# Paired rounded root sums in layer 0, and the small softmax operations taken several blocks at a time

## The chip, the cores and the metric

The kernel runs on one core of one Trainium2 chip. The metric is the device time of one execution in microseconds (us). Three runs of the kernel before took 2031.17 to 2031.62 us, median 2031.27 us. One further execution was recorded by the hardware profiler; it took 2031.74 us.

Names used below: PE is the matrix engine (TensorE) and PEld its loading of weights, DVE is VectorE, ACT is ScalarE, POOL is GpSimd, and SP is the engine that issues most DMAs. L428 means line 428 of the kernel in question; line numbers of the kernel before and of the changed one differ behind line 690.

## The reference

A decoder trunk of two layers on 1024 tokens of width 1024, in float32. Each layer normalizes its input, projects it once, and hands the columns to four mixers:

```python
for l in range(DEPTH):
    h = rmsnorm(x, attn_norm[l])
    proj = h @ w_in[l]
    (c_q, c_kv, k_r, g_b, g_c, u_conv, u_pool, q_sw, k_sw, v_sw) = jnp.split(proj, pts, axis=-1)
    y_a = mla_attention(...)       # 4 heads, causal over all tokens
    y_b = short_gated_conv(...)
    y_c = multiscale_pool(...)
    y_d = swa_sink_attention(...)  # 4 heads, window of 128, a sink logit per head
    groups = jnp.stack([y_a, y_b, y_c, y_d], axis=2)
    # each group normalized by its own root mean square, then one output projection
    x = x + mixed @ w_o[l]
    h2 = rmsnorm(x, ffn_norm[l])
    gate, up = jnp.split(h2 @ w_gate_up[l], 2, axis=-1)
    x = x + (jax.nn.silu(gate) * up) @ w_down[l]
return rmsnorm(x, final_norm)

def rmsnorm(x, g):
    y = xf * lax.rsqrt(jnp.mean(xf * xf, axis=-1, keepdims=True) + RMS_EPS)
```

Two pieces matter here. Every `rmsnorm` (and the norm of each group) needs the sum of squares over channels for each token. And both attentions end in a softmax over keys; in the local one the sink joins the denominator: exp(sink - max) is added to the sum of the row.

## The kernel before

**Data.** Activations stand with channels on the 128 partitions and tokens along the free dimension, in two halves of 512 tokens (`t` = 0, 1). A product in float32 precision is made of three matmuls on operands rounded to the fast float32 format: each operand is split into a rounded part and a rest, and `mm3` (L348) adds high x high, high x low and low x high into one PSUM bank. The split itself is `split` (L368 on ACT copies and rounds, L371 on DVE subtracts; L373 and L374 do the same with a gain). `half_split` makes such a pair for one half of the tokens.

**Root sums.** The class `SumSq` collects squares of the channel blocks into one tile per half (`add`: the square on ACT, L412, the addition on DVE, L414 and L420). `rnorm` then sums over partitions with a matmul against a matrix of ones and forms the reciprocal root (L437 to L443 on ACT and DVE). It has two forms (L428 and L431). If the object was made with `pair`, the last `add` splits the collected tile into a rounded pair, and `rnorm` uses two matmuls in the fast format:

```python
            if t in self.hl:
                for i, h in enumerate(self.hl.pop(t)):
                    pe.matmul(p, ones_r, R.ap(h), start=i == 0, stop=i == 1)
                    R.free(h)
            else:
                pe.matmul(p, ones, a, start=True, stop=final is None)
```

Otherwise it uses one matmul in plain float32. Before the change, layer 0 uses the plain form for its input norm (`ss`), the norm of the query rank (`sq_q`) and the norms of the groups c (pooling) and d (local attention); everything else is paired but for the last half of the final norm.

**Local attention.** For each of two pairs of heads (`g`) and each of eight blocks of 128 queries (`i`), `swa_unit` makes the scores of two heads against two blocks of keys (L685), adds the bias and takes the row's negative maximum (L695, a custom DVE operation), takes Exp with row sums on ACT (L708), and then, for the two heads of that block, makes the sink's part (L718 on DVE, L719 Exp on ACT), adds it (L720) and takes the reciprocal (L721). Then the rows are scaled (L723), transposed by PE (L734), split, and multiplied with the values (L746). `swa_some` calls units in between the projections, three or two at a time.

**Latent attention.** There are eight steps, one for each head `h` and half `t`. `scores` handles the four query blocks of a step: scores into PSUM (L1071 to L1073), maxima (L1076, L1079), Exp with row sums on ACT (L1090, L1093), for `t` = 1 the sum of the two partial row sums (L1102), a reciprocal (L1103), and the scaling of the rows (L1107 on ACT, L1109 on DVE). `mix_values` transposes the rows (L1125) and multiplies them with the values (L1137); it is called one step later, behind the scores of the next step.

**Order.** The program is written once in plain order, recorded, and then ordered anew by a list scheduler in the kernel (class `Order`): it gives every instruction a cost and its dependences, ranks them, and fixes an order on each engine, and with it the PSUM bank of each product and the place of each temporary. A change in the recorded instructions so moves the order of the whole program.

Of the kernel before, what the change touches and what calls it, by code (L numbers as in the profile page):

```python
# [16 lines left out]
AF = mybir.ActivationFunctionType  # L17
ALU = mybir.AluOpType
AX = mybir.AxisListType

P = 128
D = 1024
# [3 lines left out]
NK = D // P  # L26
# [100 lines left out]
def trunk_kernel(ctx: ExitStack, tc: tile.TileContext, ins, out, given=None, ends=None):  # L127
    nc = tc.nc
    act, dve, pe, pool, sp = nc.scalar, nc.vector, nc.tensor, nc.gpsimd, nc.sync
# [61 lines left out]
    def small(n):  # L191
        return spool.tile([P, n], F32, name=f"sm{n}", tag=f"sm{n}", bufs=16 if n < 16 else 2)
# [262 lines left out]
    tl = slice(64, 128)  # L455

    x_in = ins["xT"]
    ss = SumSq(D)
    hh = [[None, None] for _ in range(NK)]
    xf = [[None, None] for _ in range(NK)]  # L460
    ratt = [None, None]
# [56 lines left out]
    for l in range(L):  # L518
# [57 lines left out]
        if l == 0:  # L576
# [44 lines left out]
            for i in range(L):  # L621
                for o, c, n in ((nsink, PC_SINK, 4), (nffn, PC_FFN, NK)):
                    dve.tensor_scalar(
                        out=o[:, i * n : i * n + n],
                        in0=par[:, i * PC_N + c : i * PC_N + c + n],
                        scalar1=-1.0,
                        scalar2=None,
                        op0=ALU.mult,
# [27 lines left out]
        for t in range(2):  # L656
            f = tmp()
            mul_to(f, pv_[t], r_of(t))
            p = ps("t")
# [3 lines left out]
            for g in range(2):  # L663
# [3 lines left out]
                    out=o[:, :, 1, :], in0=pv[:, :, g, :], in1=rd(o[:, :, 0, :]), op=ALU.subtract  # L667
# [3 lines left out]
        ytiles("d")  # L671
        psy_of = {}

        def swa_unit(g, i):

            t, b = divmod(i, 4)
            lo_k = max(i - 1, 0) * P
            nkb = 2 if i else 1
            c0 = 0 if i else P
            p = ps("s")  # L680
            s3 = p.rearrange("p (h k) -> p h k", h=2)
            for h in range(2):
                q = R.ap(qs[2 * g + h][t])[:, b * P : (b + 1) * P]
                for n in range(2):
                    pe.matmul(  # L685
                        s3[:, h, c0:],
                        q,
                        R.ap2(kk[g][n])[:, lo_k : lo_k + nkb * P],
                        start=n == 0,
                        stop=n == 1,  # L690
                    )
            nm, rs = small(2), small(2)
            for h in range(2):
                c = CC_SWA + (2 * g + h) * 256
                dve.tensor_tensor_reduce(  # L695
                    out=s3[:, h, c0:],
                    in0=s3[:, h, c0:],
                    in1=cst[:, c + c0 : c + 256],
                    scale=-1.0,
                    scalar=nsink[:, l * 4 + 2 * g + h : l * 4 + 2 * g + h + 1],  # L700
                    op0=ALU.add,
                    op1=ALU.min,
                    accum_out=nm[:, h : h + 1],
                )
            pr = tmp("tp")
            p3 = pr.rearrange("p (h k) -> p h k", h=2)
            for h in range(2):
                act.activation(  # L708
                    p3[:, h, c0:],
                    s3[:, h, c0:],  # L710
                    AF.Exp,
                    bias=nm[:, h : h + 1],
                    scale=-1.0,
                    accum_out=rs[:, h : h + 1],
                )
            es = small(2)
            sk = par[:, l * PC_N + PC_SINK + 2 * g : l * PC_N + PC_SINK + 2 * g + 2]
            dve.tensor_tensor(out=es, in0=nm, in1=sk, op=ALU.add)  # L718
            act.activation(es, es, AF.Exp)  # L719
            dve.tensor_tensor(out=rs, in0=rs, in1=es, op=ALU.add)  # L720
            dve.reciprocal(rs, rs)  # L721
            for h in range(2):
                dve.tensor_scalar(  # L723
                    out=p3[:, h, c0:],
                    in0=p3[:, h, c0:],
                    scalar1=rs[:, h : h + 1],
                    scalar2=None,
                    op0=ALU.mult,
                )
            pt = ps("t")  # L730
            ptv = pt.rearrange("p (b h q) -> p b h q", b=2, h=2)
            for kb in range(2 - nkb, 2):
                for h in range(2):
                    pe.transpose(ptv[:, kb, h, :], p3[:, h, kb * P : (kb + 1) * P], ident)  # L734
            a0 = (2 - nkb) * 256
            th, tlo = R.half(), R.half()
            split(R.ap(th)[:, a0:], R.ap(tlo)[:, a0:], pt[:, a0:])
            if i % 2 == 0:
                psy_of[g] = ps("pv")
            py = psy_of[g]  # L740
            n = 0
            for kb in range(2 - nkb, 2):
                j = i - 1 + kb
                v = R.ap(vs[g][j // 4])[:, (j % 4) * P : (j % 4 + 1) * P]
                for tt in (th, tlo):
                    pe.matmul(  # L746
                        py[:, (i % 2) * 256 : (i % 2 + 1) * 256],
                        v,
                        R.ap(tt)[:, kb * 256 : (kb + 1) * 256],
                        start=n == 0,  # L750
                        stop=n == 2 * nkb - 1,
                    )
                    n += 1
            R.free(th)
            R.free(tlo)
            if i % 2:
                pyv = py.rearrange("p (i h q) -> p i h q", i=2, h=2)
                tt = tmp("tn")
                for h, rows in ((0, hd), (1, tl)):
                    tv = tt[rows, 0:256].rearrange("p (i q) -> p i q", i=2)  # L760
                    o = F.ap(y["d"][g][t])[rows, (b - 1) * P : (b + 1) * P]
                    act.copy(tv, pyv[tl, :, h, :])
                    dve.tensor_tensor(
                        out=o.rearrange("p (i q) -> p i q", i=2),
                        in0=pyv[hd, :, h, :],
                        in1=tv,
                        op=ALU.add,
                    )

        units = deque((g, i) for g in range(2) for i in range(NK))  # L770

        def swa_some(n):
            for _ in range(n):
                if units and qs[2 * units[0][0]][1] is not None:
                    g, i = units.popleft()
                    swa_unit(g, i)
                    if i == NK - 1:
                        for h in range(2):
                            for t in range(2):
                                R.free(qs[2 * g + h][t])  # L780
                        for n2 in range(2):
                            R.free_pair(kk[g][n2])
                            R.free(vs[g][n2])

        def group_scale(g):

            sg = SumSq(2 * P, g in ("b", "bcd")[l])
            for t in range(2):
                for c in range(2):
                    sg.add(t, F.ap(y[g][c][t]))  # L790
                r = sg.rnorm(t)
                for c in range(2):
                    a = F.ap(y[g][c][t])
                    mul_to(a, a, F.ap(r))
                F.free(r)
# [59 lines left out]
        for ct in range(2):  # L855
            pp = nextp
            u, a, b = F.pair(), F.pair(), F.pair()
# [16 lines left out]
            else:  # L874
# [7 lines left out]
                out=dst,  # L882
                in0=src,
                scalar=cst[:, CC_INVW + ct : CC_INVW + ct + 1],
                in1=uf,
                op0=ALU.mult,
# [7 lines left out]
            for t in range(2):  # L894
                h, lo = half_split(dst[:, t * HT : (t + 1) * HT])
                p = ps("t")
# [15 lines left out]
                rope.append(F.half())  # L912
                sp.dma_start(F.ap(rope[-1]), ins[name][:, t * HT : (t + 1) * HT])
        cq = [[None, None], [None, None]]
        sq_q = SumSq(2 * P, l > 0)
        for m in range(2):
            pp = project() if m else nextp
            for t in range(2):
# [20 lines left out]
        for t in range(2):  # L939
            p = ps("s")  # L940
# [17 lines left out]
            p = ps("t")  # L958
# [88 lines left out]
        def scores(h, t, q):  # L1047
            pr = []
            own = [F.half(), F.half(), F.half()]

            diag = ((own[0], 0), (own[1], 0), (own[0], P), (own[2], 0))
            for b in range(4):
                i = 4 * t + b
                bs = slice(b * P, (b + 1) * P)
                nch = t + 1
                wd = (b + 1) * P
                s, c = diag[b]
                chunks = [F.ap(s)[:, c : c + wd]]
                if t:
                    own.append(F.half())  # L1060
                    chunks.insert(0, F.ap(own[-1]))
                rs = small(2)
                nm = small(1)
                pts = []
                for c in range(nch):
                    w_ = HT if c < t else max((b + 1) * P, 256)
                    p = ps("s")
# [6 lines left out]
                if nch == 2:  # L1074
# [5 lines left out]
                    out=pts[t][:, :wd],  # L1080
# [17 lines left out]
                    scale=-1.0,  # L1098
                    accum_out=rs[:, 0:1],
                )  # L1100
                if nch == 2:
                    dve.tensor_tensor(out=rs[:, 0:1], in0=rs[:, 0:1], in1=rs[:, 1:2], op=ALU.add)  # L1102
                dve.reciprocal(rs[:, 0:1], rs[:, 0:1])  # L1103
                for c in range(nch):
                    a = chunks[c]
                    if c < t and b % 2:
                        act.activation(a, a, AF.Copy, scale=rs[:, 0:1])  # L1107
                        continue
                    dve.tensor_scalar(  # L1109
                        out=a, in0=a, scalar1=rs[:, 0:1], scalar2=None, op0=ALU.mult  # L1110
                    )
                pr.append(chunks)
            R.free(q[0])
            R.free(q[1])
            return pr, own
# [594 lines left out]
        for f in range(3, NFF):  # L1710
# [5 lines left out]
            if f % 2:  # L1716
                g = f // 2
# [682 lines left out]
```

## Time and profile before

| | |
|---|---|
| median of three runs | 2031.27 us |
| profiled execution | 2031.74 us, its span 2030.0 us |
| PE busy | 2018.6 us (99%) |
| DVE busy | 1531.2 us (75%) |
| ACT busy | 1022.6 us (50%) |
| POOL busy | 567.5 us (28%) |
| mean granted clock of PE | 0.999 |

The span runs from the first to the last instruction; the execution's own time holds 1.7 us more around it. The mixers of layer 0 lie between 0 and about 380 us, its feed-forward part up to about 1050 us, the mixers of layer 1 between 1050 and 1400 us, and its feed-forward part behind them. A busy PE means that matmuls are under way, not that they start at the greatest pace: ends of matmuls are modelled, so what one costs is read from the distance between starts. The mean of a group of DVE or ACT operations is the duration of one, and two that follow one another may overlap in part. Waits are inferred from semaphores; where a wait is for several, the last one is named.

### The profile page before, as it was taken

What the parts mean: (1) busy time and instruction counts of PE and PEld (TensorE: products, weight loads), DVE (VectorE), ACT (ScalarE), POOL (GpSimd) and SP (SyncE); (2) the same over time, 40 slices, a digit from 0 to 9 for tenths busy, and PEclk for the clock granted to TensorE, in tenths of its full rate; (3) what the DMA queues carried; (4) which work ended last, traced back from release to release, by engine and by line L of the source; (5) the groups of instructions that cost most, each with busy time, mean ns of one, the idle gap of its engine ahead of it and who ended that gap; (6) DMA issues with size and microseconds to landing.
All of it is one profiled execution on the core that took longest, in us unless ns stands there. A gap on an engine that the chain in (4) does not pass through costs nothing.

```text
span 2030.0 us, 26831 instructions
## 1 busy us (share of the span) xinstructions
PE 2018.6 (99%) x9418; PEld 1676.7 (83%) x9418; DVE 1531.2 (75%) x2442; ACT 1022.6 (50%) x1778; POOL 567.5 (28%) x428
## 2 busy tenths in 40 slices
PE   9999999999999999999999999999999999999998
PEld 7888888888888888888888888888888888888887
DVE  8779989997666678776646998799976766785554
ACT  7447657843333335555633676677333333354343
POOL 0100000057776772000001000000587677710000
PEclk9999999999999999999999999999999999999999
DMA  5431132336445547998835224332554554487552
GB/s 207 109 63 55 64 108 81 136 131 205 169 164 201 175 163 266 354 371 283 296 100 133 63 91 133 105 126 93 175 168 169 199 172 169 162 301 259 190 178 84
DMA packets 154232, 338.57 MB, mean 167 GB/s; under 512 B 14960, under 2 KB 62192, under 8 KB 154096
## 3 DMA queue, kind: packets, MB, share of 16 engines
q1 hardware_dynamic: 149616, 325.31, 46.6%
q0 software_dynamic: 4480, 11.54, 3.2%
q8 instruction: 74, 1.21, 0.2%
q14 instruction: 62, 0.51, 0.1%
HBM read 241.36 MB, written 105.91 MB: 171 GB/s over the span
## 4 chain that ended last, share of the span: by engine, by line
PE 96%; DVE 0%; DMA 0%; ACT 0%; issue 0%; DVEq 0%; ACTq 0%
PE ps_mm L348 37%; PE ps_s L348 30%; PE ps_t L348 12%; PE ps_pv L348 8%; PE ps_pv L1137 2%; PE ps_t L1125 1%; PE ps_s L1071 1%; PE ps_s L1072 1%; PE ps_s L1073 1%; PE ps_s L685 1%; PE ps_s L943 1%; PE ps_pv L746 1%; PE ps_t L734 1%; PE ps_t L428 0%; DMA xp<-u 0%; PE ps_t L431 0%
## 5 line engine op out<-in xcount | busy, mean ns | idle before, releaser
L348 PE MATMUL ps_mm<-u,u 128*128 128x512 f32 (+1 forms) x3378 | 833.2, 390 | 0.5 <-ACT u L368 0.3
L348 PEld LDWEIGHTS ps_mm<-u,u 128*128 128x128 f32 x3378 | 614.6, 188 | 122.7 <-issue 2.6
L371 DVE TENSOR_TENSOR u<-u,u 128x1024 fp32r<-128x1024 f32 (+3 forms) x453 | 511.3, 1148 | 194.1 <-ACT u L368 176.5
L348 PE MATMUL ps_s<-u,u 128*128 128x512 f32 x2670 | 634.0, 389 | 0.0
L348 PEld LDWEIGHTS ps_s<-u,u 128*128 128x128 f32 x2670 | 501.0, 188 | 104.9 <-issue 0.5
L368 ACT CAST u<-u 128x1024 fp32r<-128x1024 f32 (+3 forms) x453 | 385.2, 868 | 382.9 <-DMA u<-ad 73.9
L348 PE MATMUL ps_t<-u,u 128*128 128x512 f32 (+1 forms) x1124 | 254.4, 377 | 0.0
L348 PEld LDWEIGHTS ps_t<-u,u 128*128 128x128 f32 x1124 | 202.7, 188 | 39.3 <-issue 0.5
L1548 POOL TENSOR_TENSOR tm<-tm,u 128x512 f32<-128x512 f32 x80 | 139.5, 1744 | 341.6 <-ACT tm L1546 337.1
L348 PE MATMUL ps_pv<-u,u 128*128 128x512 f32 x744 | 177.5, 389 | 0.0
L348 PEld LDWEIGHTS ps_pv<-u,u 128*128 128x128 f32 x744 | 139.5, 188 | 29.1 <-ACT u L1364 0.2
L322 POOL DMA_DIRECT2D gd<-in_w_gu x24 | 21.6, 898 | 415.0 <-PE ps_t L348 281.4
L1134 POOL MEMSET u<- 128x128 f32 x32 | 6.1, 217 | 428.7 <-PE ps_mm L348 193.5
L1546 ACT ACTIVATE tm<-tm 128x512 f32<-128x512 f32 x80 | 50.6, 632 | 135.8 <-DVE tm L449 135.7
L368 ACT CAST u<-ps_t 128x512 fp32r<-128x512 f32 (+3 forms) x132 | 65.8, 504 | 54.1 <-PE ps_t L1125 27.0
L371 DVE TENSOR_TENSOR u<-ps_t,u 128x512 fp32r<-128x512 f32 (+3 forms) x132 | 75.7, 582 | 18.9 <-ACT u L368 17.2
L1414 ACT COPY tm<-ps_s 128x512 f32<-128x512 f32 x61 | 35.8, 587 | 101.7 <-PE ps_s L348 101.6
L1626 POOL TENSOR_TENSOR u<-u,u 128x352 f32<-128x352 f32 x64 | 81.4, 1272 | 1.4
L412 ACT ACTIVATE tm<-u 128x512 f32<-128x512 f32 (+1 forms) x91 | 53.9, 600 | 49.2 <-DVE u L1817 41.2
L373 ACT ACTIVATE u<-u,par 128x512 fp32r<-128x512 f32 x99 | 69.4, 715 | 17.8 <-DVE u L1274 7.6
L1626 POOL TENSOR_TENSOR u<-u 128x352 f32<-128x352 f32 x64 | 75.4, 1180 | 3.0 <-DMA u<-in_w_dn 2.8
L374 DVE SCALAR_TENSOR_TENSOR u<-u,par,u 128x512 fp32r<-128x512 f32 x99 | 72.5, 745 | 4.4 <-ACT u L373 4.1
(206 smaller groups left out, 2316.3 us busy)
## 6 DMA issues: line engine op xcount, KB each, us to landing
u<-in_w_gu SPq DMA_DIRECT2D x84, 512.0 KB, 4.1
ad<-u SPq DMA_DIRECT2D x154, 256.0 KB, 3.2
u<-ad SPq DMA_DIRECT2D x70, 512.0 KB, 5.9
u<-in_w_dn SPq DMA_DIRECT2D x64, 352.0 KB, 3.4
qd<-u SPq DMA_DIRECT2D x64, 352.0 KB, 2.5
u<-in_w_in SPq DMA_DIRECT2D x43, 512.0 KB, 5.8
u<-qd SPq DMA_DIRECT2D x32, 512.0 KB, 5.4
u<-in_w_dn SPq DMA_DIRECT2D x24, 512.0 KB, 5.4
```

What stands on the lines that cost most here:

```text
L322: paced(pool.dma_start(d, a, **more))
L348: last_mm = pe.matmul(o, w, r, start=start and k == 0 and i == 0, stop=stop and k == n - 1 and i == 2, skip_group_check=again,)
L368: a = act.copy(hi, f)
L371: dve.tensor_tensor(out=lo, in0=f, in1=rd(hi), op=ALU.subtract)
L373: a = act.activation(hi, f, AF.Copy, scale=gain)
L374: dve.scalar_tensor_tensor(out=lo, in0=f, scalar=gain, in1=rd(hi), op0=ALU.mult, op1=ALU.subtract)
L412: act.activation(q, f, AF.Square)
L1137: pe.matmul(py[:, c0:], v_of(j, h), R.ap(s)[:, c0:], start=j == 0 and n == 0, stop=j == nj - 1 and n == 1,)
L1414: act.copy(o, p)
L1546: last_silu = act.activation(g, g, AF.Silu)
L1548: pool.tensor_tensor(out=g, in0=g, in1=r, op=ALU.mult)
L1626: pool.tensor_tensor(out=o, in0=a, in1=b, op=ALU.add)
```

## The change

Three places change what is computed in which instruction; the result is the same sum, maximum and quotient.

- In layer 0 the input norm, the query norm and the norms of groups c and d use the paired form of the root sum.
- In the local attention two neighbouring blocks are one unit: `swa_pair` makes the scores of both (`swa_scores`), does the sink's part, the addition and the reciprocal for four columns (two blocks of two heads) at once, and then goes on with each block (`swa_values`). `swa_some` counts what it owes and calls a pair for every two.
- In the latent attention the row sums of the four blocks of a step stand in one small tile; the addition and the reciprocal are done once for the step, and all scaling follows.

```diff
@@ -455,7 +455,7 @@
     tl = slice(64, 128)
 
     x_in = ins["xT"]
-    ss = SumSq(D)
+    ss = SumSq(D, True)
     hh = [[None, None] for _ in range(NK)]
     xf = [[None, None] for _ in range(NK)]
     ratt = [None, None]
@@ -671,7 +671,7 @@
         ytiles("d")
         psy_of = {}
 
-        def swa_unit(g, i):
+        def swa_scores(g, i, nm, rs):
 
             t, b = divmod(i, 4)
             lo_k = max(i - 1, 0) * P
@@ -689,7 +689,6 @@
                         start=n == 0,
                         stop=n == 1,
                     )
-            nm, rs = small(2), small(2)
             for h in range(2):
                 c = CC_SWA + (2 * g + h) * 256
                 dve.tensor_tensor_reduce(
@@ -713,12 +712,30 @@
                     scale=-1.0,
                     accum_out=rs[:, h : h + 1],
                 )
-            es = small(2)
+            return p3
+
+        def swa_pair(g, i):
+
+            nm, rs, es = small(4), small(4), small(4)
+            ps_ = [swa_scores(g, i + n, nm[:, 2 * n :], rs[:, 2 * n :]) for n in range(2)]
             sk = par[:, l * PC_N + PC_SINK + 2 * g : l * PC_N + PC_SINK + 2 * g + 2]
-            dve.tensor_tensor(out=es, in0=nm, in1=sk, op=ALU.add)
+            dve.tensor_tensor(
+                out=es.rearrange("p (i h) -> p i h", i=2),
+                in0=nm.rearrange("p (i h) -> p i h", i=2),
+                in1=sk.unsqueeze(1).to_broadcast([P, 2, 2]),
+                op=ALU.add,
+            )
             act.activation(es, es, AF.Exp)
             dve.tensor_tensor(out=rs, in0=rs, in1=es, op=ALU.add)
             dve.reciprocal(rs, rs)
+            for n in range(2):
+                swa_values(g, i + n, ps_[n], rs[:, 2 * n :])
+
+        def swa_values(g, i, p3, rs):
+
+            t, b = divmod(i, 4)
+            nkb = 2 if i else 1
+            c0 = 0 if i else P
             for h in range(2):
                 dve.tensor_scalar(
                     out=p3[:, h, c0:],
@@ -767,14 +784,16 @@
                         op=ALU.add,
                     )
 
-        units = deque((g, i) for g in range(2) for i in range(NK))
+        units, owed = deque((g, i) for g in range(2) for i in range(0, NK, 2)), [0]
 
         def swa_some(n):
-            for _ in range(n):
+            owed[0] += n
+            while owed[0] > 1:
+                owed[0] -= 2
                 if units and qs[2 * units[0][0]][1] is not None:
                     g, i = units.popleft()
-                    swa_unit(g, i)
-                    if i == NK - 1:
+                    swa_pair(g, i)
+                    if i == NK - 2:
                         for h in range(2):
                             for t in range(2):
                                 R.free(qs[2 * g + h][t])
@@ -784,7 +803,7 @@
 
         def group_scale(g):
 
-            sg = SumSq(2 * P, g in ("b", "bcd")[l])
+            sg = SumSq(2 * P, True)
             for t in range(2):
                 for c in range(2):
                     sg.add(t, F.ap(y[g][c][t]))
@@ -912,7 +931,7 @@
                 rope.append(F.half())
                 sp.dma_start(F.ap(rope[-1]), ins[name][:, t * HT : (t + 1) * HT])
         cq = [[None, None], [None, None]]
-        sq_q = SumSq(2 * P, l > 0)
+        sq_q = SumSq(2 * P, True)
         for m in range(2):
             pp = project() if m else nextp
             for t in range(2):
@@ -1049,6 +1068,7 @@
             own = [F.half(), F.half(), F.half()]
 
             diag = ((own[0], 0), (own[1], 0), (own[0], P), (own[2], 0))
+            sums8 = small(8)
             for b in range(4):
                 i = 4 * t + b
                 bs = slice(b * P, (b + 1) * P)
@@ -1059,7 +1079,7 @@
                 if t:
                     own.append(F.half())
                     chunks.insert(0, F.ap(own[-1]))
-                rs = small(2)
+                rs = sums8[:, 2 * b : 2 * b + 2]
                 nm = small(1)
                 pts = []
                 for c in range(nch):
@@ -1098,18 +1118,22 @@
                     scale=-1.0,
                     accum_out=rs[:, 0:1],
                 )
-                if nch == 2:
-                    dve.tensor_tensor(out=rs[:, 0:1], in0=rs[:, 0:1], in1=rs[:, 1:2], op=ALU.add)
-                dve.reciprocal(rs[:, 0:1], rs[:, 0:1])
-                for c in range(nch):
-                    a = chunks[c]
+                pr.append(chunks)
+            both = sums8.rearrange("p (b c) -> p b c", c=2)
+            inv = small(4)
+            if t:
+                dve.tensor_tensor(out=inv, in0=both[:, :, 0], in1=both[:, :, 1], op=ALU.add)
+                dve.reciprocal(inv, inv)
+            else:
+                dve.reciprocal(inv, both[:, :, 0])
+            for b, chunks in enumerate(pr):
+                for c, a in enumerate(chunks):
                     if c < t and b % 2:
-                        act.activation(a, a, AF.Copy, scale=rs[:, 0:1])
+                        act.activation(a, a, AF.Copy, scale=inv[:, b : b + 1])
                         continue
                     dve.tensor_scalar(
-                        out=a, in0=a, scalar1=rs[:, 0:1], scalar2=None, op0=ALU.mult
+                        out=a, in0=a, scalar1=inv[:, b : b + 1], scalar2=None, op0=ALU.mult
                     )
-                pr.append(chunks)
             R.free(q[0])
             R.free(q[1])
             return pr, own
```

The order around these places moves as follows. First PE at the query norm of layer 0, among the projections (`ps_mm`) of the gated convolution and the pooling: `ones_r` is the matrix of ones, the other `u` names are slots of activations and weights. Before:

```order
L348 MATMUL ps_mm<-u_358,u_1831 128x512
L431 MATMUL ps_t<-u_1928,ones_r 128x512
L348 MATMUL ps_mm<-u_370,u_1830 128x512 x2
L348 MATMUL ps_mm<-u_370,u_1831 128x512
L348 MATMUL ps_mm<-u_382,u_1830 128x512 x2
```

and of the change:

```order
L348 MATMUL ps_mm<-u_386,u_1796 128x512 x2
L348 MATMUL ps_mm<-u_386,u_1797 128x512
L428 MATMUL ps_t<-u_1901,ones_r 128x512
L348 MATMUL ps_s<-u_1721,vhi 128x512 x2
L348 MATMUL ps_s<-u_1721,vlo 128x512
```

One plain root has become two matmuls of the pair (the first of them stands six matmul rows further up, outside of this piece), and they stand further back among the projections.

Next DVE at the first local-attention blocks of layer 0, where `sm` are the small tiles of maxima and sums and ISA is the custom operation of bias and maximum. Before:

```order
L695 ISA ps_s,sm_568<-ps_s,cst,nsink 128x128
L695 ISA sm_568 128x1
L243 TENSOR_TENSOR u_1018<-u_1015,u_1017 128x1024
L718 TENSOR_TENSOR sm_575<-sm_568,par 128x2
L243 TENSOR_TENSOR vlo<-vraw,vhi 128x256
L720 TENSOR_TENSOR sm_569<-sm_569,sm_575 128x2
L721 RECIPROCAL sm_569<-sm_569 128x2
L449 TENSOR_TENSOR u_502<-ps_mm,u_308 128x512
L695 ISA ps_s,sm_596<-ps_s,cst,nsink 128x256
L695 ISA sm_596 128x1
L723 TENSOR_SCALAR tm<-tm,sm_569 128x128 x2
```

and of the change:

```order
L694 ISA ps_s,sm_571<-ps_s,cst,nsink 128x256
L694 ISA sm_571 128x1
L722 TENSOR_TENSOR sm_573<-sm_571,par 128x4
L243 TENSOR_TENSOR u_998<-u_995,u_997 128x1024
L729 TENSOR_TENSOR sm_572<-sm_572,sm_573 128x4
L730 RECIPROCAL sm_572<-sm_572 128x4
L740 TENSOR_SCALAR tm<-tm,sm_572 128x128 x2
L740 TENSOR_SCALAR tm<-tm,sm_572 128x256 x2
```

The three small operations stand once behind the second block's maxima, four columns wide, and the first block's scaling has moved behind them.

Last DVE in a step of the latent attention of layer 1 with two key halves (`t` = 1). Before, from its second block on:

```order
L1102 TENSOR_TENSOR sm_11635<-sm_11635 128x1
L1103 RECIPROCAL sm_11635<-sm_11635 128x1
L1109 TENSOR_SCALAR u_11614<-u_11614,sm_11635 128x256
L1079 ISA ps_s,sm_11656<-ps_s,cst,sm_11665 128x384
L1079 ISA sm_11656 128x1
L1076 TENSOR_REDUCE sm_11684<-ps_s 128x1
L371 TENSOR_TENSOR u_11716<-ps_t,u_11716 128x256
L1177 TENSOR_TENSOR u_8094<-u_8094,ps_mm 128x512
L1102 TENSOR_TENSOR sm_11655<-sm_11655 128x1
L1103 RECIPROCAL sm_11655<-sm_11655 128x1
L1079 ISA ps_s,sm_11675<-ps_s,cst,sm_11684 128x512
```

and of the change, the end of the same step:

```order
L1099 ISA ps_s,sm_11510<-ps_s,cst,sm_11519 128x512
L1099 ISA sm_11510 128x1
L1201 TENSOR_TENSOR u_8018<-u_8018,ps_mm 128x512
L1177 TENSOR_TENSOR u_7284<-ps_pv,tm 64x512
L1125 TENSOR_TENSOR sm_11524<-sm_11465 128x4
L1126 RECIPROCAL sm_11524<-sm_11524 128x4
L1134 TENSOR_SCALAR u_11466<-u_11466,sm_11524 128x512
L1134 TENSOR_SCALAR u_11495<-u_11495,sm_11524 128x512
L1134 TENSOR_SCALAR u_7284<-u_7284,sm_11524 128x128
L1134 TENSOR_SCALAR u_11464<-u_11464,sm_11524 128x256
```

The additions and reciprocals of the four blocks have become one of each behind the last block's maximum, and the scaling of all four follows them without a break.

## The prediction

> **What bounds the kernel now.** I read the page's totals and chain first, then the busy time of the engines by stage, then the waits of TensorE.
>
> ```profile
> span 2030.0 us, 26831 instructions
> PE 2018.6 (99%) x9418; PEld 1676.7 (83%) x9418; DVE 1531.2 (75%) x2442; ACT 1022.6 (50%) x1778; POOL 567.5 (28%) x428
> PE 96%; DVE 0%; DMA 0%; ACT 0%; issue 0%; DVEq 0%; ACTq 0%
> ```
>
> TensorE (PE) is busy for 99% of the span and is 96% of the chain that ended last. Only two things can then move the time: work that PE itself no longer has, or waits of PE that come or go. By stage (length, then busy time and count of PE, PEld, DVE, ACT, POOL):
>
> ```profile
> 0.00:50.00 50.00, 48.41 (x211) 38.48 (x211) 44.16 (x73) 39.96 (x67) 1.94 (x6) 1.00 0.59 208
> 150.00:200.00 50.00, 50.00 (x230) 39.74 (x229) 47.93 (x96) 39.08 (x77) 0.00 (x0) 1.00 0.15 48
> 200.00:350.00 150.00, 150.00 (x784) 126.26 (x783) 132.38 (x321) 95.93 (x226) 3.00 (x16) 1.00 0.24 80
> 380.00:1050.00 670.00, 670.00 (x2961) 554.51 (x2959) 477.18 (x539) 305.84 (x416) 273.20 (x185) 1.00 0.62 218
> 1200.00:1350.00 150.00, 149.41 (x776) 124.34 (x776) 126.47 (x313) 97.27 (x225) 3.10 (x16) 1.00 0.32 103
> ```
>
> The feed-forward stage (380 to 1050) has PE without a gap, and the change does not touch it. In the stages it does touch, VectorE (DVE) is the near second bound: 96% busy from 150 to 200, 88% and 84% in the two latent-attention stages. All waits of PE that the profile shows:
>
> ```profile
> PE ps_pv L579 <- DVE ones_r L198: 1.3, 1, 1.3
> PE ps_s L435 <- ACT tm L434: 0.5, 1, 0.5
> PE ps_mm L348 <- ACT u L368: 0.3, 1, 0.3
> PE ps_mm L348 <- DVE u L374: 0.2, 1, 0.2
> PE ps_t L1125 <- ACT u L1093: 0.2, 1, 0.2
> PE ps_s L1071 <- ACT u L1093: 0.2, 1, 0.2
> PE ps_s L685 <- DVE u L666: 0.2, 1, 0.2
> ```
>
> The first two are the start and the tail, which stay. The other five are 1.1 us. A matmul's modelled end lies later than the start of the next one (0.39 us long, 0.227 us apart, below), so each wait hides about 0.17 us more: 1.1 + 5 x 0.17 = 2.0 us. That is all that lighter helpers can give.
>
> **Part one: the roots of layer 0.** The unpaired root sum (line 431) becomes two matmuls of rounded halves (line 428). How many there are, and the pace of PE when nothing holds it (from the chain):
>
> ```profile
> L431 PE MATMUL ps_t<-u,ones_r x16: 590/592/688, 19.2 to 195.4; 128*128 128x512 f32 x16
> 386.94 8.16 PE ps_s L348 x36
> ```
>
> Each float32 root is recorded as two instructions, so 16 records are eight roots, all before 195.4 us, in layer 0: two of the input norm, two each of group scales c and d, two of the query norm. The pace is 8.16 / 36 = 0.2267 us a matmul. The price of a root comes from the starts around it (timeline of PE: start, length, what):
>
> ```profile
> 190.40 1.02 PE L431 MATMUL ps_t<-u,ones_r 128*128 128x512 f32 x2
> 190.85 4.24 PE L348 MATMUL ps_mm<-u,u 128*128 128x512 f32 x16
> 194.93 1.02 PE L431 MATMUL ps_t<-u,ones_r 128*128 128x512 f32 x2
> 195.39 6.26 PE L348 MATMUL ps_mm<-u,u 128*128 128x512 f32 x25
> 201.49 0.28 PE L1071 MATMUL ps_s<-u,u 128*128 128x256 f32 x1
> ...
> 381.77 0.40 PE L428 MATMUL ps_pv<-u,ones_r 128*128 128x512 f32 x1
> 382.01 1.30 PE L348 MATMUL ps_mm<-u,u 128*128 128x512 f32 x5
> 383.14 0.40 PE L428 MATMUL ps_pv<-u,ones_r 128*128 128x512 f32 x1
> ```
>
> From 190.40 to 194.93 stand one root and 16 matmuls: 4.53 - 16 x 0.2267 = 0.90 us. From 194.93 to 201.49, 6.56 - 25 x 0.2267 = 0.89 us. A half of a paired root: 1.37 - 5 x 0.2267 = 0.24 us, so the pair takes 0.47 us. The difference is 0.42 us. It holds some lateness of the matmuls behind, which I allow 0.04 us for at the low end (0.38). I take 0.40, and eight roots give **-3.2 us** (-3.0 to -3.4), all on the bound engine.
>
> What the pairs add is a split for each root, one rounding copy on ACT and one subtraction on DVE:
>
> ```profile
> L368 ACT CAST u<-u 128x512 fp32r<-128x512 f32 x117 | 72.3, 619 | 104.5 <-DVE u L891 28.5 <-POOL u L1336 19.6 <-POOL u L1626 14.1
> L371 DVE TENSOR_TENSOR u<-u,u 128x512 fp32r<-128x512 f32 x117 | 97.8, 839 | 26.6 <-ACT u L368 25.9 <-PE ps_mm L348 0.4
> ```
>
> That is 8 x 0.62 = 5.0 us of ACT and at most 8 x 0.84 = 6.7 us of DVE in layer 0, and 1.5 us more from a root's last sum to its first matmul. Cover: projections, which the order puts in front of the root. If that cover is gone, the delay is PE's (second rival). The matmul side of the weights is no cost: PEld is busy 83%.
>
> **Part two: the small operations.** Counts and lengths (shortest, median, longest in ns), as the lines' own views give them:
>
> ```profile
> L718 DVE TENSOR_TENSOR sm<-sm,par x32: 138/153/162, 53.4 to 1166.8; 128x2 f32<-128x2 f32 x32
> L719 ACT ACTIVATE sm<-sm x32: 187/200/232, 53.6 to 1167.9; 128x2 f32<-128x2 f32 x32
> L721 DVE RECIPROCAL sm<-sm x32: 152/160/168, 54.1 to 1168.4; 128x2 f32<-128x2 f32 x32
> L1102 DVE TENSOR_TENSOR sm<-sm x32: 138/152/160, 241.5 to 1327.5; 128x1 f32<-128x1 f32 x32
> L1103 DVE RECIPROCAL sm<-sm x64: 141/156/166, 208.6 to 1341.3; 128x1 f32<-128x1 f32 x64
> ```
>
> In the local attention each of three DVE operations (lines 718, 720, 721) and the Exp on ACT go from 32 to 16: 48 fewer on DVE, 16 on ACT. In the latent attention the sums go from 32 to 8 and the reciprocals from 64 to 16: 72 fewer. What one occupies:
>
> ```profile
> 1271.99 0.16 DVE L1102 TENSOR_TENSOR sm<-sm 128x1 f32<-128x1 f32 x1 [0.34 <-ACT u L1093]
> 1272.18 0.16 DVE L1103 RECIPROCAL sm<-sm 128x1 f32<-128x1 f32 x1
> 1272.38 0.49 DVE L1109 TENSOR_SCALAR u<-u,sm 128x512 f32<-128x512 f32 x1
> ```
>
> They follow at 0.19 to 0.20 us, one behind the other, and DVE also stood idle for 0.34 us in front of the first one. So 120 operations are 120 x 0.153 = 18 us by their length, or 24 us by their spacing, half of it in each layer. Operations four wide instead of one or two have no row; from the same 0.15 us at one and two wide I take no change. Net of the splits, DVE loses 2 to 5 us of work in layer 0 and 9 to 12 us in layer 1; ACT gets 5.0 - 16/2 x 0.2 = 3.4 us more work in layer 0 and 1.6 us less in layer 1.
>
> None of this is PE's own work, so its worth lies between nothing and the 2.0 us of waits. The profile shows that not all of those are DVE's to give: the wait at line 1071 goes back past ACT to a store of the output projection:
>
> ```profile
> 1271.50 0.37 ACT L1093 ACTIVATE u<-ps_s,sm 128x128 f32<-128x128 f32 x1 [0.44 <-DMA xp<-u]
> ```
>
> I take a quarter, **-0.5 us**, because two of the five name DVE, and waiting for a whole step may cost something back at other places. The order also has the transposes in fewer, longer runs; I count nothing for it.
>
> The trace's 18 to 24 us has a counterpart in the Trainium skill, Perfetto Trace Analysis, section Optimizing Scalar/DVE Operations: it puts the engine-busy overhead of a DVE operation on SBUF at about 60 ns. By that figure the 120 operations would be worth an estimated 7 us, about what the splits cost; the rows show two to three times as much, and I go by them.
>
> **The sum.** The profiled execution took 2031.74 us (span 2030.0, 1.7 around it), 0.47 us over the median of 2031.27. 2031.74 - 3.2 - 0.5 = 2028.0 in a profiled execution; less 0.47 it is **2027.6 us** for the median.
>
> **Rivals.** *The batches free PE wholly.* DVE in the latent attention is 84 to 88% busy, with idle time in front of small operations that wait for ACT in line. If shorter queues bring every late operand in time, all 2.0 us go: 2031.3 - 3.2 - 2.0 = 2026.1 us. For it: the bracketed wait above occurs at each block and would occur once a step. Against it: PE's waits are few and scattered, and one is a store's. 0.32.
>
> *The split chain takes the start.* The first 50 us have DVE at 44.16 of 50 and PE's wait on line 666 comes at their end. Two pairs add 2 x 0.7 us to DVE there and 1.5 us to each root's path; if DVE passes its addition on to the first local-attention scores, PE waits 1.4 us more: 2029.0 us. Against it: the second root's operands have projections before them. 0.12.
>
> *The last block holds the first (slower).* Now a block's scale follows its own Exp; afterwards none is scaled before the fourth. In the last step of a layer no later scores cover this. The trace there (four reciprocals, first and last, then PE's first transposes of that step):
>
> ```profile
> 334.09 0.15 DVE L1103 RECIPROCAL sm<-sm 128x1 f32<-128x1 f32 x1
> ...
> 339.12 0.17 DVE L1103 RECIPROCAL sm<-sm 128x1 f32<-128x1 f32 x1 [0.24 <-ACT u L1093]
> ...
> 342.46 0.60 PE L1125 MATMUL ps_t<-cst,u 128*128 128x128 f32 x4
> ```
>
> A first block is held for up to 5.0 us. PE's transposes come 3.3 us after the last reciprocal anyway, so the cover is there now. It decides against the change from 3.7 us of new waits, that is 0.23 us in each of 16 steps; at the full 5.0 us in both last steps it costs 10 us less 3.7: 2037.6 us. 0.06, most of it at smaller sizes. The Trainium skill has a rule on this side (Perfetto Trace Analysis, Optimizing Scalar/DVE Operations): where ACT or DVE are not saturated but cause bubbles elsewhere, breaking up instructions may finish work sooner, and grouping pays where the engine is saturated. With PE's wait total above, the trace so far shows hardly a bubble for it to act on.
>
> That the order, drawn anew for the whole program, gives no gain on the roots would need new waits of 3.2 us; it is in the last two rivals.
>
> **How the numbers follow.** Forecast 0.50, rivals 0.32, 0.12 and 0.06. About 0.2% (4.1 us) is what a measurement of this kernel can tell from no change; that bound lies at 2027.2 us, only 0.4 below the forecast. Faster by more: the first rival, and a fifth of the forecast's cases, 0.42. Slower by more than 0.2%: 0.04, from the last rival. Within: the rest, 0.54. The forecast's own range is 2026.8 to 2028.6 (root price, half of the waits either way). The range takes in the first two rivals: 2025.3 to 2030.0 us.
>
> **What would show it.** Line 431 should keep only the tail's records, and the two matmuls of a root should stand 0.47 us on PE. DVE busy should fall by 11 to 17 us, and PE's waits between 50 and 1400 us should be no more than now. New waits of the transposes of the step or of the local attention on DVE or ACT in 50 to 350 would prove the sum wrong, as would a PE busy time that fell by less than 2.5 us.

## The result and the profile after

The changed kernel took 2028.18 us (median of 20 runs, 2027.36 to 2029.15) against 2031.62 us of the kernel before (20 runs, 2030.82 to 2032.88). The ratio is 0.9982, 95% interval 0.9976 to 0.9988: 3.4 us faster, just inside the 0.2% that was called no change; the interval reaches over that bound. 2027.6 us was predicted. (All times are medians; one of all executions here and below, of the kernel with reciprocals put back, took 2891 us for a cause that is not known, and the median does not feel it.)

The totals of the changed kernel's page, then its engines' busy time in the stretches that were shown of before:

```profile
span 2026.6 us, 26712 instructions
PE 2015.0 (99%) x9418; PEld 1679.6 (83%) x9418; DVE 1521.4 (75%) x2330; ACT 1023.4 (50%) x1770; POOL 570.3 (28%) x428
```

```profile
0.00:50.00 50.00, 48.53 (x214) 40.62 (x215) 44.13 (x73) 40.85 (x68) 1.94 (x6) 1.00 0.62 208
150.00:200.00 50.00, 50.00 (x236) 41.36 (x235) 48.89 (x91) 39.43 (x75) 0.00 (x0) 1.00 0.14 45
200.00:350.00 150.00, 149.11 (x781) 125.37 (x780) 133.00 (x290) 98.84 (x230) 3.02 (x16) 1.00 0.27 86
1200.00:1350.00 150.00, 150.00 (x780) 125.73 (x779) 122.76 (x275) 94.75 (x222) 2.88 (x16) 1.00 0.31 99
```

PE lost 3.6 us of busy time (2018.6 to 2015.0), the span 3.4 us. In layer 0 DVE is as full as before, in 31 fewer instructions between 200 and 350; in layer 1 its busy time fell by 3.7 us between 1200 and 1350. The waits of PE, and the two forms of the root:

```profile
PE ps_pv L579 <- DVE ones_r L198: 1.3, 1, 1.3
PE ps_mm L348 <- DVE tm L449: 0.9, 1, 0.9
PE ps_s L435 <- ACT tm L434: 0.5, 1, 0.5
```

```profile
L431 PE MATMUL ps_s<-u,ones_r x4: 378/378/378, 1999.6 to 2016.5; 128*128 128x256 f32 x4
...
L428 PE MATMUL ps_t<-u,ones_r x56: 390/397/498, 21.1 to 1397.7; 128*128 128x512 f32 x56
```

The plain root is left in the tail alone, and line 428 has 16 records more under `ps_t` (56 for 40). The five scattered waits are gone; one of 0.9 us is new, at 227 us, where PE waits for a DVE operation that reads a bank of products (line 449) and stands behind the split of an earlier tile. What a pair takes in layer 0 (timeline of PE):

```profile
182.84 3.82 PE L348 MATMUL ps_mm<-u,u 128*128 128x512 f32 x16
186.50 0.40 PE L428 MATMUL ps_t<-u,ones_r 128*128 128x512 f32 x1
186.74 2.01 PE L348 MATMUL ps_mm<-u,u 128*128 128x512 f32 x8
188.58 0.40 PE L428 MATMUL ps_t<-u,ones_r 128*128 128x512 f32 x1
188.82 0.62 PE L348 MATMUL ps_s<-u,vhi 128*128 128x512 f32 x2
```

Each half stands 0.24 us (186.50 to 186.74, 188.58 to 188.82), the pair 0.48 us; the plain root stood 0.89 to 0.90 us.

For the comparisons below I take PE's time apart in one way for all kernels. Its **bare work** is the number of matmuls of each shape times their undisturbed spacing (0.2267 us for 512 columns, 0.120 for 256, 0.109 for a transpose, 0.86 for a plain root): about 2003.4 us with the plain roots, 2000.1 us with the pairs, 3.3 us less. The **rest** is the time from PE's first to its last matmul start less the bare work: warm-up, the tail, switches between forms, and every wait, also those too short to leave a gap behind a modelled end. The level of both depends on the spacings taken, so only differences between kernels are used. Before, the rest was 16.4 us (2019.8 us between the first and the last start); in the changed kernel it is 16.3 us (2016.5 us). So by this count the whole gain is as large as the roots' work, and the rest is the same in sum. Whether that is what each edit is worth is another question.

### The profile page after: what moved, and what is told of

The parts are those of the page before. It is cut to its first block, busy times and chain, and to the rows that moved or that the text cites. A ratio compares the mean times of both kernels' runs of the same rounds, so it can differ in the third digit from the quotient of the medians.

```text
span 2026.6 us, 26712 instructions
## 1 busy us (share of the span) xinstructions
PE 2015.0 (99%) x9418; PEld 1679.6 (83%) x9418; DVE 1521.4 (75%) x2330; ACT 1023.4 (50%) x1770; POOL 570.3 (28%) x428
## 4 chain that ended last, share of the span: by engine, by line
PE 98%; ACT 1%; DVE 0%; DMA 0%; issue 0%; DVEq 0%; ACTq 0%
PE ps_mm L348 38%; PE ps_s L348 30%; PE ps_t L348 12%; PE ps_pv L348 8%; PE ps_pv L1161 2%; PE ps_t L1149 2%; PE ps_s L1091 1%; PE ps_s L1092 1%; PE ps_s L1093 1%; PE ps_s L962 1%; PE ps_pv L763 1%; PE ps_s L685 1%; PE ps_t L428 1%; PE ps_t L751 1%; DMA u<-in_w_gu 0%; ACT u L368 0%
## 5 line engine op out<-in xcount | busy, mean ns | idle before, releaser
L368 ACT CAST u<-u 128x1024 fp32r<-128x1024 f32 (+3 forms) x461 | 389.4, 864 | 376.4 <-DMA u<-ad 68.6
L1360 POOL TENSOR_TENSOR u<-u 128x512 f32<-128x512 f32 x38 | 68.1, 1793 | 39.7 <-DVE u L371 39.7
```

What stands on the lines that cost most here:

```text
L368: a = act.copy(hi, f)
L1360: pool.tensor_tensor(out=q4, in0=q4, in1=F.ap(self.raw[1] + 1), op=ALU.add)
```

## The experiments

All comparisons are in five rounds against the kernel before; the interval of a ratio is about 0.0009 wide to either side, which is 1.8 us. (The kernel before had a median of 2031.78 or 2031.49 us in these rounds; ratios go by those, and the table at the end by the 2031.62 us above.) Since the scheduler orders the whole program anew for every kernel, three orders were taken of each: the one it finds as it is, one with another seed of its search, and one with other stretch factors of its costs.

**The roots alone.**

```diff
-    ss = SumSq(D)
+    ss = SumSq(D, True)
-            sg = SumSq(2 * P, g in ("b", "bcd")[l])
+            sg = SumSq(2 * P, True)
-        sq_q = SumSq(2 * P, l > 0)
+        sq_q = SumSq(2 * P, True)
```

> Only the roots of layer 0 are paired; the softmax operations stay one block at a time. Theory A (the roots carry the gain, since they are PE's own work): 3.0 to 3.4 us less than before, ratio 0.9985 (0.9983 to 0.9988). Rival B (the batches carry a good part of it, the splits eat some of the roots' gain): 1.0 to 2.2 us less, ratio 0.9989 to 0.9995. Both expect line 431 without its records of layer 0 and DVE busier than before by 5 us or more.

2036.20 us (11 runs), ratio 1.0022 (1.0013 to 1.0031): 4.4 us *slower*. Neither theory had that. The totals, and the longest of PE's waits between start and tail:

```profile
PE 2020.5 (99%) x9418; PEld 1674.3 (82%) x9418; DVE 1551.9 (76%) x2450; ACT 1026.7 (50%) x1786; POOL 561.7 (28%) x428
```

```profile
PE ps_t L734 <- ACT vhi L242: 1.0, 1, 1.0
PE ps_t L348 <- DVE u L1355: 0.9, 2, 0.7
PE ps_mm L348 <- DVE tm L449: 0.7, 1, 0.7
PE ps_mm L348 <- ACT u L1093: 0.6, 1, 0.6
```

The rest is 24.4 us, 8.0 more than before, which is more than the roots' 3.3. The longest wait is at the first block of the local attention; PE, then DVE ahead of it:

```profile
54.71 3.35 PE L348 MATMUL ps_mm<-u,u 128*128 128x512 f32 x14
59.08 0.43 PE L734 MATMUL ps_t<-cst,tm 128*128 128x128 f32 x2 [1.02 <-ACT vhi L242]
```

```profile
57.41 0.15 DVE L720 TENSOR_TENSOR sm<-sm,sm 128x2 f32<-128x2 f32 x1
57.58 0.16 DVE L718 TENSOR_TENSOR sm<-sm,par 128x2 f32<-128x2 f32 x1
57.66 0.49 DVE L695 CUSTOM_DVE_ANT_0 ps_s<-ps_s,cst,nsink 128x256 f32<-128x256 f32 x1
58.06 0.14 DVE L695 DVE_READ_ACCUMULATOR2_ANT sm<- 128x1 f32 x1
58.06 0.16 DVE L721 RECIPROCAL sm<-sm 128x2 f32<-128x2 f32 x1
58.24 0.49 DVE L695 CUSTOM_DVE_ANT_0 ps_s<-ps_s,cst,nsink 128x256 f32<-128x256 f32 x1
58.65 0.14 DVE L695 DVE_READ_ACCUMULATOR2_ANT sm<- 128x1 f32 x1
58.65 0.48 DVE L723 TENSOR_SCALAR tm<-tm,sm 128x128 f32<-128x128 f32 x2
```

PE has run out of projections at 57.9 us, and the rows that it is to transpose are scaled from 58.65 on. The first scaling ended at 58.93 us and the ACT copy that the wait names at 58.99, so which of them held PE is not shown; both came late. DVE has not stopped: its sums and reciprocals stand between the maxima of the next block. In the changed kernel the same place has no gap:

```profile
53.46 4.73 PE L348 MATMUL ps_mm<-u,u 128*128 128x512 f32 x20
58.03 0.38 PE L751 MATMUL ps_t<-cst,tm 128*128 128x128 f32 x2
```

```profile
56.51 0.16 DVE L729 TENSOR_TENSOR sm<-sm,sm 128x4 f32<-128x4 f32 x1
56.70 0.18 DVE L730 RECIPROCAL sm<-sm 128x4 f32<-128x4 f32 x1
56.92 1.01 DVE L740 TENSOR_SCALAR tm<-tm,sm 128x128 f32<-128x128 f32 x4
```

One set of small operations serves both blocks, the scaling begins at 56.92, and PE has 20 projections in front of the transposes.

**The batches alone.** The changed kernel with the three lines above put back.

> Only the small softmax operations are batched; the eight roots stay plain. Theory A: 0 to 0.5 us less than before, ratio 0.9997 to 1.0001, with DVE busy 15 us or more lower than before. Rival B: 1.5 to 2.0 us less, ratio 0.9990 to 0.9993. Rival D (the batch holds PE up): 0.5 us or more slower, with new waits of PE in the attention stages.

2031.49 us, ratio 0.9998 (0.9989 to 1.0007), rest 16.0 us. In this order theory A holds for the batches. Their DVE total fell:

```profile
PE 2017.4 (99%) x9418; PEld 1678.1 (83%) x9418; DVE 1520.8 (75%) x2322; ACT 1019.3 (50%) x1762; POOL 569.3 (28%) x428
```

That is 10.4 us less than before, where 15 were expected.

**Another seed, of the changed kernel and of the kernel before.**

```diff
-        draw = random.Random(1)
+        draw = random.Random(2)
```

> The changed kernel with another seed of the random search in its scheduler: the same instructions in another order. It shows how much the order alone moves the time. If the one new wait of PE of 0.9 us in the changed kernel (at 227 us, on the product with the rope table) belongs to its order and not to its instructions, it is absent here and the time is up to 1 us under the changed kernel. If the order is worth little, the time is within 0.5 us of it: ratio to before 0.9980 to 0.9985.

2029.39 us, ratio 0.9990 (0.9981 to 0.9999). That is 1.2 us over the changed kernel with the first seed, where 0.5 at most was expected, but inside the uncertainty. The wait of 0.9 us at line 449 is still there, so the seed did not remove it.

> The kernel before with the other seed of its scheduler's search: the same instructions in another order. Theory A takes the difference of the kernels as that of their instructions, so this should be within 0.7 us of the kernel before (ratio 0.9997 to 1.0003). If it moves by 1.5 us or more, the order is worth as much as half of the change, and a term of 0.5 us can't be told from it.

2032.11 us, ratio 1.0001 (0.9992 to 1.0010): no difference. But seeds share the plan that the search starts from; they are no independent draws.

**The single edits with the other seed.**

> The kernel with the paired roots alone, with another seed of its scheduler's search. With the first seed it took 2036.2 us, 4.4 over the kernel before, and its waits of PE were spread over all stages. Theory E (the splits load DVE and ACT in layer 0, and without the batches the waits come with any order): again 2034 us or more, ratio 1.001 or more. Theory F (that order was a bad draw): 2028 to 2030 us, ratio 0.9983 to 0.9992, where the 3.2 us of the roots show.

2035.99 us, ratio 1.0019 (1.0011 to 1.0028), rest 23.9 us: the loss comes again.

> The kernel with the batches alone, with the other seed. Theory A: within 1 us of the kernel before again (ratio 0.9995 to 1.0005). If it comes out at 2029 us or less, the batches are worth over 2 us and the first seed hid it; at 2033 us or more, the batches alone are a loss.

2029.72 us, ratio 0.9990 (0.9981 to 0.9998), rest 14.0 us: between the bounds set, near the one at which the batches are worth over 2 us.

**Small operations put back into the chain.** The changed kernel with 144 more reciprocals on DVE, in front of the scaling. Each set is even in number, so the value stays, up to rounding.

```diff
-            dve.reciprocal(rs, rs)
+            for _ in range(5):
+                dve.reciprocal(rs, rs)
...
+            for _ in range(6 if t else 4):
+                dve.reciprocal(inv, inv)
             for b, chunks in enumerate(pr):
```

> The changed kernel with reciprocals of reciprocals put behind each batched reciprocal (an even number, so the value stays): 144 more small operations on DVE, in the chain to the scaling, more than the 112 that the change takes away net. If the load of small operations on DVE is what keeps PE waiting (Theory E), the gain goes: 2031 us or more, ratio 0.9998 or more. If the small operations are hidden wherever they stand and only the draw of the order counts (Theory F), it stays within 1.2 us of the changed kernel: ratio 0.9980 to 0.9990.

2031.37 us, ratio 0.9999 (0.9990 to 1.0008): the gain is gone. The rest rose from 16.3 to 19.5 us with PE's bare work unchanged. The totals, and one set on DVE:

```profile
PE 2018.3 (99%) x9418; PEld 1676.7 (83%) x9418; DVE 1555.0 (77%) x2474; ACT 1023.0 (50%) x1770; POOL 569.1 (28%) x428
```

```profile
57.84 1.03 DVE L731 RECIPROCAL sm<-sm 128x4 f32<-128x4 f32 x5
```

Small operations on DVE are thus not free in a kernel whose PE is 99% busy; 144 of them cost 3.2 us here. Whether by the time that they take on DVE or by holding the scaling behind them (five take 1.03 us in place of 0.18), this run can't tell, and the order was drawn anew for it too.

**Roots, with only the local attention batched.** The changed kernel with `scores` as before.

> Paired roots and paired blocks in the local attention; the latent attention keeps a sum and a reciprocal for each block. Theory E puts the relief where DVE is fullest, in the local attention beside the splits (0 to 200 us): 2028 to 2030 us, ratio 0.9982 to 0.9992. If the relief of the latent attention is the one that counts: 2032 us or more. Theory F expects anything from 2028 to 2033 us.

2032.64 us, ratio 1.0004 (0.9996 to 1.0013), rest 20.5 us. Against the roots alone 3.6 us come from the local attention's pairs, and another 4.5 us lie between this and the full change, which adds the latent attention's batch. By what was written down this is the outcome in which the latent attention's relief counts; but the two parts are alike in size, so Theory E's place for the relief was too narrow.

**All four kernels in an order found from another start.**

```diff
-SLOW = (1.0, 1.03)
+SLOW = (1.015, 1.045)
```

> The kernel before, with the scheduler's two stretch factors for DVE and ACT costs set to 1.015 and 1.045 in place of 1.0 and 1.03: the same instructions, in an order found from another start, not only by another seed. It says how far the order alone moves the time. Theory F (the draw of the order decides about the last microseconds): 1.5 us or more away from the kernel before. Theory E (waits follow the load): within 1 us, ratio 0.9995 to 1.0005.

2035.20 us, ratio 1.0016 (1.0007 to 1.0025): 3.6 us more than the kernel before, with the same instructions.

> The changed kernel with the same other stretch factors. Theory E: 3 to 4 us under the kernel of the same factors without the change. Theory F: anywhere between 2026 and 2031 us.

2029.17 us, ratio 0.9987 (0.9978 to 0.9996): 6.0 us under the kernel before in the same order, more than Theory E's 3 to 4, and inside Theory F's bounds.

> Paired roots alone with the other stretch factors. Theory E (the pairs' splits, without the batches, bring waits of more than the 3.2 us they save): again 2 us or more over the kernel before of the same factors. Theory F (two bad draws, of one start): up to 3.2 us under it.

2032.23 us, ratio 1.0002 (0.9993 to 1.0011): here the roots alone are 3.0 us under their own kernel without them. That is Theory F's outcome.

> The batches alone with the other stretch factors. With it all four kernels (neither edit, either, both) stand in three orders each. From the two orders so far (0.3 and 1.8 us less than before): 0 to 2 us under the kernel before of the same factors.

2029.88 us, ratio 0.9991 (0.9982 to 1.0000): 5.3 us under its own kernel before, more than was expected.

All four kernels in the three orders, medians in us, with the rest of PE (from one profiled execution each) in brackets:

| | first order | other seed | other stretch |
|---|---|---|---|
| neither | 2031.62 (16.4) | 2032.11 (19.0) | 2035.20 (19.2) |
| roots | 2036.20 (24.4) | 2035.99 (23.9) | 2032.23 (20.7) |
| batches | 2031.49 (16.0) | 2029.72 (14.0) | 2029.88 (14.5) |
| both | 2028.18 (16.3) | 2029.39 (16.7) | 2029.17 (17.3) |

Both against neither: 3.4, 2.7 and 6.0 us less. The batches on top of the roots: 8.0, 6.6 and 3.1 us less, each time beyond the uncertainty (no run of the one kernel reaches into those of the other). The batches without the roots: 0.1, 2.4 and 5.3 us less. The roots without the batches: 4.6 and 3.9 more, then 3.0 less. The roots on top of the batches: 3.3, 0.3 and 0.7 us less, the last two inside the uncertainty. The roots always take 3.3 us of bare work away; what a median moves beyond that is rest. By the medians the roots so add 7.9, 7.2 and 0.3 us of rest without the batches, and 0.0, 3.0 and 2.6 with them. (The brackets alone would give 8.0, 4.9 and 1.5 for the first three: the profiled execution of neither edit with the other seed took 2034.38 us, 2.3 over its median, and as much more rest lies in its first feed-forward part.)

Where the rest lies can be read from the same traces, by taking window by window the time less the bare work that started in it. The mixers of layer 0 (0 to 380 us) are the only stage to which the pairs add splits; the batches act in the mixers of both layers (0 to 380 and 1050 to 1400 us). Differences of the rest in us:

| | first order | other seed | other stretch |
|---|---|---|---|
| roots without the batches, layer 0 | +4.5 | +4.6 | +2.0 |
| roots with the batches, layer 0 | +0.9 | +1.9 | +2.6 |
| batches without the roots, both layers | -1.2 | -3.6 | -4.0 |
| batches with the roots, both layers | -6.4 | -6.2 | -2.4 |

Of the 8.0 us that the roots alone add in the first order, 3.5 lie behind 380 us, where the kernel has the instructions of the kernel before: that part is the order's and not the splits'.

Theory E in its weak form fits: where the splits of the pairs load DVE and ACT, the rest grows in every order, and in two of three most of that is gone with the batches. The roots without the batches are a loss in those two orders, which share a start. Theory F is right as to the size: the same instructions moved by 3.6 us from one order to another. None of the versions run is faster than the changed kernel.

## Why the prediction was right, and where not

**The total** came out 0.6 us from the forecast, inside its own narrow range, and 3.4 us were gained where 3.7 were forecast. The call of no change clear of 0.2% was right, as the ratio's 0.18% is just short of it. For the parts that is luck: in the order that was forecast -3.3 us of roots, 7.9 us of new rest with them and -8.0 us of the batches add up to -3.4, and the last two terms stood in the sum as 0 and -0.5. In the other two orders the same change gave 2.7 and 6.0 us.

**The roots' work** was right: eight roots, 0.42 us each by the rows, -3.2 us taken. The rows after give 0.41 to 0.42 us (0.48 against 0.89 to 0.90), 3.3 us for eight.

**The splits' cover** was called the projections in front of the root, with 1.4 us if it fails at the start. That step failed for the roots alone. Without the batches the rest grew by 0.3 to 7.9 us by the medians, and in the mixers of layer 0 by 2.0 to 4.6 us. I costed a split by the path to its root; that it puts everything behind it on DVE and ACT later fits the rows at 58 us above, but is not shown apart from the order drawn anew: in the first order the rest between 1050 and 1400 us, where no split was added, was 1.6 us larger too. The second rival named the start: in the first 100 us the roots alone did add 1.3, 1.5 and 1.2 us of rest in the three orders, near its 1.4. It left out the stages behind, and that the other edit can pay for it: with the batches the same difference is -1.0, -0.1 and 2.2 us.

**The batches** were put at -0.5 us out of a bound of 2.0 us. The bound was wrong. It was made of the five waits that the view shows and 0.17 us for each; by the starts of PE's matmuls the waits longer than 0.02 us came to about 5.4 us in some 50 places (the count moves a little with the spacing taken as undisturbed), since those shorter than the overhang of the modelled end are not shown at all. By themselves the batches gave 0.1 us in the first order, no more than the term, but 2.4 and 5.3 in the others; on top of the roots they gave 3.1 to 8.0 us, six to sixteen times the term. The sum came right because the splits' cost, put at nothing, was as large.

**The first rival** (all waits go) did not occur in this order, as the rest stayed at 16.3 us. With the other seed and the other factors the batches alone gave its 2.0 us and more, but not to the last wait: 14.0 and 14.5 us of rest are left.

**The last rival** (a step's first block held by its last) did not show as a loss: PE's waits on the step's transposes are gone from the view (shorter ones it would not show), and the four-wide operations cost nearly the same, 0.15 to 0.18 us each. The sum and the reciprocal of a step in the changed kernel:

```profile
L1125 DVE TENSOR_TENSOR sm<-sm x8: 155/164/165, 242.7 to 1325.3; 128x4 f32<-128x4 f32 x8
...
L1126 DVE RECIPROCAL sm<-sm x8: 169/178/178, 243.4 to 1325.5; 128x4 f32<-128x4 f32 x8
```

The Trainium skill says that breaking up instructions may let work finish sooner where ACT or DVE are not saturated but cause bubbles elsewhere (Perfetto Trace Analysis, Optimizing Scalar/DVE Operations); no loss of that kind shows here. The Trainium skill also says that grouping can improve throughput if the engine is saturated. The batches on top of the roots agree with that in all three orders (3.1 to 8.0 us), though DVE was not full throughout: it was 74 to 96% busy before in the stages concerned.

**The signs named.** Line 431 kept only the tail's records and PE's busy time fell by 3.6 us, as said. DVE's busy time fell by 9.8 us where 11 to 17 were said. One new wait of 0.9 us showed in 50 to 350 us, on DVE, but in front of a projection and not of the transposes that were named; in sum PE's shown waits were no more than before (0.9 against 1.1 us). So of the signs only DVE's total spoke against the sum, and none showed that two of its terms were far off.

**What stays open:** how much of the roots' extra rest is load and how much the luck of the order. Three orders, two of which share a start, are too few, and the orders were not held fixed while the instructions changed. So the gain of the change is shown, and that the batches lower the time of the kernel with pairs; why they do, by DVE's load or by the order, is in part argued.

## What to carry to other kernels

Where one engine is busy throughout, as PE is here, an edit that moves work from it to the helpers has two prices, the work it saves and the waits that the helpers then cause; cost the second from how full they are in that stage, not from the path of the edited operation alone, and pair such an edit with one that unloads them. A list of waits that shows little does not say that there is little: take the distance between starts against the undisturbed pace. And where a scheduler orders a whole program anew, try an edit in more than one order before a gain of a few microseconds is put down to it.

## What the runs showed that was not expected

The same instructions in another order took 3.6 us more (2035.20 against 2031.62 us), as much as the whole change. And 144 operations of about 0.17 us on DVE, about 0.21 us apart and so 30 us in sum, cost 3.2 us with PE 99% busy, about a tenth of their own time.
